# Batch norm on one core: loads and stores on two DMA rings, parameters in 16 equal rows, a shared last tile, and channels dealt 16 x 8 to the partitions

## The chip, the cores and the metric

One core of one Trainium2 chip. The metric is the device time of the kernel in microseconds (us), as the median of several runs. "The span" is the time from the first to the last record of one profiled execution; it is some 2 us shorter than the timed run. SBUF is the core's on-chip memory, rows of it are called partitions (128 of them); HBM is the large memory that x and the output lie in. A transfer (DMA) is cut into packets, here mostly one 64 KB row each, which 16 DMA engines carry; a ring is a queue of transfers for these engines (q1, SyncE's, and q10, ScalarE's, in the profiles). "In flight" means begun and not yet ended.

## The reference

```python
# x: (32, 256, 128, 128) float32; the parameters have one value per channel, shape (256,)
return gamma * (x - running_mean) / np.sqrt(running_var + 1e-5) + beta
```

Per channel this is one multiplication and one addition: `x * scale + shift`. x and the output have 536.9 MB each, so the kernel is a stream through the core.

## The kernel before

One image and 128 channels make a tile: 128 partitions x 16384 values, 64 KB per partition, 8.39 MB. There are 64 tiles and three buffers. All loads and stores are issued by SyncE, so they stand in one DMA ring (q1, 99.9% of the engines' span): three loads, three stores, three loads.

```python
NBUF = 3
GROUPS = [3] * 20 + [2, 2]
xr = x.rearrange("n (cb p) h w -> (n cb) p (h w)", p=P)          # partition p holds channel cb*128 + p
outr = out.rearrange("n (cb p) h w -> (n cb) p (h w)", p=P)

def load(i):
    t = data.tile([P, HW], f32, tag="t")
    nc.sync.dma_start(out=t[:], in_=xr[i])
    tiles[i] = t
# parameters: one row each, from ScalarE's ring, then a transpose and copies to 128 partitions
for r, ap in enumerate((running_var, gamma, beta, running_mean)):
    nc.scalar.dma_start(out=rows[r : r + 1, :], in_=ap.rearrange("(o c) -> o c", o=1))
# ... scale_t and shift_t from them: 12 small instructions (cut) ...
def compute(i):                       # in place, on VectorE
    nc.vector.tensor_scalar(out=t[:], in0=t[:], scalar1=scale_t[:, cb : cb + 1],
                            scalar2=shift_t[:, cb : cb + 1], op0=mult, op1=add)
first = 0
for g, size in enumerate(GROUPS):
    idxs = range(first, first + size)
    for i in idxs: compute(i)
    for i in idxs: store(i)           # nc.sync.dma_start(out=outr[i], in_=t[:])
    first += size
    for i in range(first, min(first + more, NT)): load(i)   # more: the size of the next group
```

Of the kernel before, what the change touches and what calls it, by code (L numbers as in the profile page):

```python
# [1 line left out]

# [4 lines left out]


NBUF = 3
GROUPS = [3] * 20 + [2, 2]  # L10

AHEAD = 0


@with_exitstack
def kernel(
    ctx: ExitStack,
    tc: tile.TileContext,
    x: bass.AP,
    gamma: bass.AP,  # L20
    beta: bass.AP,
    running_mean: bass.AP,
    running_var: bass.AP,
    out: bass.AP,
):
    nc = tc.nc
    eps = 1e-5
    f32 = mybir.dt.float32

    N, C, H, W = x.shape  # L30
    P = nc.NUM_PARTITIONS
    assert C % P == 0
    NCB = C // P
    HW = H * W
    NT = N * NCB
    B = 32
    NQ = P // B
    assert sum(GROUPS) == NT and max(GROUPS) <= NBUF

    params = ctx.enter_context(tc.tile_pool(name="params", bufs=1))  # L40
    data = ctx.enter_context(tc.tile_pool(name="data", bufs=NBUF))

    xr = x.rearrange("n (cb p) h w -> (n cb) p (h w)", p=P)
    outr = out.rearrange("n (cb p) h w -> (n cb) p (h w)", p=P)

    ctx.enter_context(tc.manual_schedule())
    tiles = {}

    def load(i):
        t = data.tile([P, HW], f32, tag="t")  # L50
        nc.sync.dma_start(out=t[:], in_=xr[i])  # L51
        tiles[i] = t


    rows = params.tile([B, C], f32, tag="rows")
    nc.vector.memset(rows, 0.0)  # L56
    for r, ap in enumerate((running_var, gamma, beta, running_mean)):
        nc.scalar.dma_start(out=rows[r : r + 1, :], in_=ap.rearrange("(o c) -> o c", o=1))

    for i in range(AHEAD + GROUPS[0]):  # L60
        load(i)

    eps_t = params.tile([P, 1], f32, tag="eps")
    nc.vector.memset(eps_t, eps)  # L64
    turned = params.tile([B, C], f32, tag="turned")
    nc.vector.transpose(out=turned[:], in_=rows[:])  # L66

    par = params.tile([P, NCB, 4], f32, tag="par")
    blocks = turned.rearrange("p (cb q r) -> p cb q r", cb=NCB, q=NQ)
    for q in range(NQ):  # L70
        nc.vector.tensor_copy(out=par[q * B : (q + 1) * B], in_=blocks[:, :, q, 0:4])  # L71
    var_t, gamma_t, beta_t, mean_t = (par[:, :, r] for r in range(4))

    scale_t = params.tile([P, NCB], f32, tag="scale")
    shift_t = params.tile([P, NCB], f32, tag="shift")
    tmp_t = params.tile([P, NCB], f32, tag="tmp")

    nc.scalar.activation(  # L78
        out=tmp_t[:],
        in_=var_t,  # L80
        func=mybir.ActivationFunctionType.Sqrt,
        bias=eps_t[:],
        scale=1.0,
    )
    nc.vector.reciprocal(out=tmp_t[:], in_=tmp_t[:])  # L85
    nc.vector.tensor_mul(out=scale_t[:], in0=gamma_t, in1=tmp_t[:])  # L86
    nc.vector.tensor_mul(out=tmp_t[:], in0=mean_t, in1=scale_t[:])  # L87
    nc.vector.tensor_sub(out=shift_t[:], in0=beta_t, in1=tmp_t[:])  # L88

    def compute(i):  # L90
        t = tiles[i]
        cb = i % NCB
        nc.vector.tensor_scalar(  # L93
            out=t[:],
            in0=t[:],
            scalar1=scale_t[:, cb : cb + 1],
            scalar2=shift_t[:, cb : cb + 1],
            op0=mybir.AluOpType.mult,
            op1=mybir.AluOpType.add,
        )  # L100

    def store(i):
        t = tiles.pop(i)
        nc.sync.dma_start(out=outr[i], in_=t[:])  # L104


    first = 0
    for g, size in enumerate(GROUPS):
        idxs = range(first, first + size)
        for i in idxs:  # L110
            compute(i)
        for i in idxs:
            store(i)
        first += size
        more = GROUPS[g + 1] if g + 1 < len(GROUPS) else 0
        for i in range(first + AHEAD, min(first + AHEAD + more, NT)):
            load(i)


# [1 line left out]
_INS = ['x', 'gamma', 'beta', 'running_mean', 'running_var']  # L121
_OUTS = [((32, 256, 128, 128), 'float32')]


# [23 lines left out]
```

## Time and profile before

| | before |
|---|---|
| time, median (all) | 2485.87 us (2485.76 to 2486.37; 2485.97 in the three runs that the prediction had) |
| VectorE busy | 566 us of 2483.6 |
| DMA | 99.9% of 16 engines' span, 432 GB/s |
| one 64 KB DMA packet, median | 2418 ns, loads and stores alike |
| tile load, issue to landing, median | 58.0 us (three stand in the ring) |

The large idle time of VectorE follows from the busy DMA. The lines and their reading are in the prediction.

### The profile page before, as it was taken

To read this page: it belongs to the slowest core of one execution; us is meant where nothing else is said; L and a number is where in the kernel's file an instruction comes from. 1 tells how busy PE (TensorE), PEld (TensorE's weight loads), DVE (VectorE), ACT (ScalarE), POOL (GpSimd) and SP (SyncE) were. 2 spreads that over 40 slices of the span, in tenths; PEclk is the share of its full clock that TensorE was granted. 3 is DMA by queue.
4 is the path that set the end of the run, shared out by engine and by line. 5 is a ranking of instruction groups with operands and counts; after the bars stand their busy time and mean duration, and the time that the engine had idled before them with its cause. 6 is when DMAs were issued, how large, how long until landed. Compare 5 with 4: busy or idle time off the path is not lost.

```text
span 2483.6 us, 383 instructions
## 1 busy us (share of the span) xinstructions
DVE 566.0 (23%) x75; ACT 1.6 (0%) x2; POOL 0.2 (0%) x4
## 2 busy tenths in 40 slices
DVE  3140404121221213140403121221213040403112
ACT  0000000000000000000000000000000000000000
POOL 0000000000000000000000000000000000000000
DMA  9999999999999999999999999999999999999999
GB/s 421 423 439 439 425 436 439 431 431 439 431 431 439 435 426 436 436 431 435 435 435 427 439 434 427 439 434 427 439 437 432 432 437 433 431 437 433 431 437 396
DMA packets 18442, 1073.77 MB, mean 432 GB/s; under 512 B 2052, under 2 KB 2056, under 8 KB 2056
## 3 DMA queue, kind: packets, MB, share of 16 engines
q1 hardware_dynamic: 18432, 1073.75, 99.9%
q14 instruction: 2, 0.02, 0.0%
q10 hardware_dynamic: 8, 0.00, 0.0%
HBM read 536.88 MB, written 536.87 MB: 432 GB/s over the span
## 4 chain that ended last, share of the span: by engine, by line
another core or an unknown queue 72%; DVE 22%; DMA 4%; issue 0%; DVEq 0%; SPq 0%
DVE t L93 22%; DMA t<-in_x_dram 4%; DVEq L93 0%; SPq L51 0%; SPq L104 0%
## 5 line engine op out<-in xcount | busy, mean ns | idle before, releaser
L93 DVE TENSOR_SCALAR t<-t,scale_t,shift_t 128x16384 f32<-128x16384 f32 x64 | 564.0, 8812 | 1863.9 <-DMA t<-in_x_dram 1863.8
L66 DVE STREAM_TRANSPOSE turned<-rows 32x256 f32<-32x256 f32 x1 | 0.4, 432 | 21.5 <-DMA rows<-in_running_mean_dram 21.5
L78 ACT ACT_TABLE_LOAD x1 | 1.3, 1283 | 2.6 <-issue 2.6
L71 DVE COPY par<-turned 32x8 f32<-32x8 f32 x4 | 0.6, 161 | 0.1
L56 DVE MEMSET rows<- 32x256 f32 x1 | 0.3, 272 | 0.8 <-PEq L132 0.8
L78 ACT ACTIVATE tmp_t<-par,eps_t 128x2 f32<-128x2 f32 x1 | 0.3, 297 | 20.0 <-DVE par L71 20.0
L85 DVE RECIPROCAL tmp_t<-tmp_t 128x2 f32<-128x2 f32 x1 | 0.2, 165 | 0.4 <-ACT tmp_t L78 0.4
L87 DVE TENSOR_TENSOR tmp_t<-par,scale_t 128x2 f32<-128x2 f32 x1 | 0.2, 161 | 0.0
L88 DVE TENSOR_TENSOR shift_t<-par,tmp_t 128x2 f32<-128x2 f32 x1 | 0.2, 161 | 0.0
L86 DVE TENSOR_TENSOR scale_t<-par,tmp_t 128x2 f32<-128x2 f32 x1 | 0.2, 160 | 0.0
L132 POOL MEMSET const-uint8-127<- 128x1 uint8 x1 | 0.1, 103 | 0.0
L132 POOL MEMSET const-bfloat16-1.0<- 128x1 bf16 x1 | 0.1, 101 | 0.0
L132 POOL MEMSET const-float32-0.0<- 128x1 f32 x1 | 0.1, 98 | 0.2 <-issue 0.2
L132 POOL MEMSET const-float32-1.0<- 128x1 f32 x1 | 0.1, 98 | 0.0
L64 DVE MEMSET eps_t<- 128x1 f32 x1 | 0.1, 59 | 0.0
## 6 DMA issues: line engine op xcount, KB each, us to landing
t<-in_x_dram SPq DMA_DIRECT2D x64, 58.0
out_dram<-t SPq DMA_DIRECT2D x64, 49.1
rows<-in_running_var_dram ACTq DMA_DIRECT2D x1, 1.0 KB
rows<-in_gamma_dram ACTq DMA_DIRECT2D x1, 1.0 KB
rows<-in_beta_dram ACTq DMA_DIRECT2D x1, 1.0 KB
rows<-in_running_mean_dram ACTq DMA_DIRECT2D x1, 1.0 KB
```

The lines of the kernel that those rows point to most:

```text
L56: nc.vector.memset(rows, 0.0)
L64: nc.vector.memset(eps_t, eps)
L66: nc.vector.transpose(out=turned[:], in_=rows[:])
L71: nc.vector.tensor_copy(out=par[q * B : (q + 1) * B], in_=blocks[:, :, q, 0:4])
L78: nc.scalar.activation(out=tmp_t[:], in_=var_t, func=mybir.ActivationFunctionType.Sqrt, bias=eps_t[:], scale=1.0,)
L85: nc.vector.reciprocal(out=tmp_t[:], in_=tmp_t[:])
L86: nc.vector.tensor_mul(out=scale_t[:], in0=gamma_t, in1=tmp_t[:])
L87: nc.vector.tensor_mul(out=tmp_t[:], in0=mean_t, in1=scale_t[:])
L88: nc.vector.tensor_sub(out=shift_t[:], in0=beta_t, in1=tmp_t[:])
L93: nc.vector.tensor_scalar(out=t[:], in0=t[:], scalar1=scale_t[:, cb : cb + 1], scalar2=shift_t[:, cb : cb + 1], op0=mybir.AluOpType.mult, ...
L132: nc = _bacc.Bacc("TRN2", target_bir_lowering=False, num_devices=1)
```

## The change

Its intent: (1) loads on SyncE's ring and stores on ScalarE's, so that neither stands behind the other; (2) each parameter row sent to 16 partitions, so that each engine has the same number of packets, behind the first half of tile 0; (3) the last tile shared by VectorE and ScalarE; (4) channels dealt so that partition 8e+k holds channel 16k+e: the 16 engines are meant to work on 16 adjacent rows of HBM at a time. Core of the diff:

```diff
-    xr = x.rearrange("n (cb p) h w -> (n cb) p (h w)", p=P)
-    outr = out.rearrange("n (cb p) h w -> (n cb) p (h w)", p=P)
+    NE = 16;  NK = P // NE
+    xr = x.rearrange("n (cb k e) h w -> (n cb) e k (h w)", k=NK, e=NE)
+    outr = out.rearrange("n (cb k e) h w -> (n cb) e k (h w)", k=NK, e=NE)
...
-        nc.scalar.dma_start(out=rows[r : r + 1, :], in_=ap.rearrange("(o c) -> o c", o=1))
+        nc.sync.dma_start(out=bufs[0][:, left], in_=xr[0][:, :, left]).then_inc(early, 16)
+            inst = nc.sync.dma_start(out=rows[0:NE, r * C : (r + 1) * C], in_=ap.partition_broadcast(NE))
+        nc.sync.dma_start(out=bufs[0][:, right], in_=xr[0][:, :, right]).then_inc(loaded[0], 16)
+        for i in range(1, NT):
+            s, turn = i % NBUF, i // NBUF
+            inst = nc.sync.dma_start(out=bufs[s][:], in_=xr[i]).then_inc(loaded[s], 16)
+            if turn:
+                inst._wait_ge(stored[s], 16 * turn)
...
+                out=lined.rearrange("p (rc e k) -> p rc e k", e=NE, k=NK),     # the parameters dealt likewise
+                in_=rows.rearrange("p (rc k e) -> p rc e k", k=NK, e=NE),
...
-        nc.sync.dma_start(out=outr[i], in_=t[:])
+            nc.scalar.dma_start(out=outr[i], in_=bufs[s][:])._wait_ge(done, after).then_inc(stored[s], 16)
...
+        compute(last, slice(0, VCOLS))          # VCOLS = 9216 of 16384 columns on VectorE
+        nc.scalar.activation(out=t[:, VCOLS:], in_=t[:, VCOLS:], func=Identity,
+                             bias=shift_t[:, cb : cb + 1], scale=scale_t[:, cb : cb + 1])
```

More of the change, by code (lines that the diff above doesn't have):

```diff
@@ L9 @@
 NBUF = 3
-GROUPS = [3] * 20 + [2, 2]
-AHEAD = 0
+VCOLS = 9216
 @with_exitstack
@@ L37 @@
     NQ = P // B
-    assert sum(GROUPS) == NT and max(GROUPS) <= NBUF
-    params = ctx.enter_context(tc.tile_pool(name="params", bufs=1))
-    data = ctx.enter_context(tc.tile_pool(name="data", bufs=NBUF))
-    xr = x.rearrange("n (cb p) h w -> (n cb) p (h w)", p=P)
-    outr = out.rearrange("n (cb p) h w -> (n cb) p (h w)", p=P)
-    ctx.enter_context(tc.manual_schedule())
-    tiles = {}
-    def load(i):
-        t = data.tile([P, HW], f32, tag="t")
-        nc.sync.dma_start(out=t[:], in_=xr[i])
-        tiles[i] = t
@@ L55 @@
-    rows = params.tile([B, C], f32, tag="rows")
-    nc.vector.memset(rows, 0.0)
-    for r, ap in enumerate((running_var, gamma, beta, running_mean)):
-        nc.scalar.dma_start(out=rows[r : r + 1, :], in_=ap.rearrange("(o c) -> o c", o=1))
-    for i in range(AHEAD + GROUPS[0]):
-        load(i)
-    eps_t = params.tile([P, 1], f32, tag="eps")
-    nc.vector.memset(eps_t, eps)
-    turned = params.tile([B, C], f32, tag="turned")
-    nc.vector.transpose(out=turned[:], in_=rows[:])
-    par = params.tile([P, NCB, 4], f32, tag="par")
@@ L69 @@
-    blocks = turned.rearrange("p (cb q r) -> p cb q r", cb=NCB, q=NQ)
-    for q in range(NQ):
-        nc.vector.tensor_copy(out=par[q * B : (q + 1) * B], in_=blocks[:, :, q, 0:4])
-    var_t, gamma_t, beta_t, mean_t = (par[:, :, r] for r in range(4))
-    scale_t = params.tile([P, NCB], f32, tag="scale")
-    shift_t = params.tile([P, NCB], f32, tag="shift")
-    tmp_t = params.tile([P, NCB], f32, tag="tmp")
-    nc.scalar.activation(
-        out=tmp_t[:],
-        in_=var_t,
-        func=mybir.ActivationFunctionType.Sqrt,
-        bias=eps_t[:],
-        scale=1.0,
-    )
@@ L85 @@
-    nc.vector.reciprocal(out=tmp_t[:], in_=tmp_t[:])
-    nc.vector.tensor_mul(out=scale_t[:], in0=gamma_t, in1=tmp_t[:])
-    nc.vector.tensor_mul(out=tmp_t[:], in0=mean_t, in1=scale_t[:])
-    nc.vector.tensor_sub(out=shift_t[:], in0=beta_t, in1=tmp_t[:])
-    def compute(i):
-        t = tiles[i]
-        cb = i % NCB
-        nc.vector.tensor_scalar(
-            out=t[:],
-            in0=t[:],
-            scalar1=scale_t[:, cb : cb + 1],
-            scalar2=shift_t[:, cb : cb + 1],
-            op0=mybir.AluOpType.mult,
-            op1=mybir.AluOpType.add,
-        )
@@ L102, in store @@
-    def store(i):
-        t = tiles.pop(i)
-        nc.sync.dma_start(out=outr[i], in_=t[:])
-    first = 0
-    for g, size in enumerate(GROUPS):
-        idxs = range(first, first + size)
-        for i in idxs:
-            compute(i)
-        for i in idxs:
-            store(i)
-        first += size
-        more = GROUPS[g + 1] if g + 1 < len(GROUPS) else 0
-        for i in range(first + AHEAD, min(first + AHEAD + more, NT)):
-            load(i)
+    NE = 16
+    NPAR = 4
+    NK = P // NE
@@ new lines @@
+    xr = x.rearrange("n (cb k e) h w -> (n cb) e k (h w)", k=NK, e=NE)
+    outr = out.rearrange("n (cb k e) h w -> (n cb) e k (h w)", k=NK, e=NE)
+    params = ctx.enter_context(tc.tile_pool(name="params", bufs=1))
+    data = ctx.enter_context(tc.tile_pool(name="data", bufs=1))
+    bufs = [data.tile([P, HW], f32, name=f"t{s}", tag=f"t{s}") for s in range(NBUF)]
+    rows = params.tile([B, NPAR * C], f32, name="rows", tag="rows")
+    lined = params.tile([B, NPAR * C], f32, name="lined", tag="lined")
@@ new lines @@
+    turned = params.tile([B, NPAR * C], f32, name="turned", tag="turned")
+    par = params.tile([P, NPAR, NCB], f32, name="par", tag="par")
+    eps_t = params.tile([P, 1], f32, name="eps_t", tag="eps")
+    std_t = params.tile([P, NCB], f32, name="std_t", tag="std")
+    rstd_t = params.tile([P, NCB], f32, name="rstd_t", tag="rstd")
+    scale_t = params.tile([P, NCB], f32, name="scale_t", tag="scale")
+    ms_t = params.tile([P, NCB], f32, name="ms_t", tag="ms")
+    shift_t = params.tile([P, NCB], f32, name="shift_t", tag="shift")
@@ new lines, with step, compute, store @@
+    loaded = [tc.alloc_semaphore(f"loaded{s}") for s in range(NBUF)]
+    stored = [tc.alloc_semaphore(f"stored{s}") for s in range(NBUF)]
+    early = tc.alloc_semaphore("early")
+    done = tc.alloc_semaphore("done")
+    fetched = tc.alloc_semaphore("fetched")
+    vec = tc.alloc_semaphore("vec")
+    act = tc.alloc_semaphore("act")
+    with tc.tile_critical():
+        count = [0]
+        def step(inst, sem=None, value=None):
+            if sem is not None:
+                inst._wait_ge(sem, value)
+            elif count[0]:
+                inst._wait_ge(vec, count[0])
+            inst.then_inc(vec, 1)
+            count[0] += 1
+            return count[0]
+        left, right = slice(0, HW // 2), slice(HW // 2, HW)
+        last = NT - 1
+        nc.sync.dma_start(out=bufs[0][:, left], in_=xr[0][:, :, left]).then_inc(early, 16)
+        zeroed = step(nc.vector.memset(rows[:], 0.0))
+        for r, ap in enumerate((running_var, gamma, beta, running_mean)):
+            inst = nc.sync.dma_start(out=rows[0:NE, r * C : (r + 1) * C], in_=ap.partition_broadcast(NE))
+            if r == 0:
+                inst._wait_ge(vec, zeroed)
+            inst.then_inc(fetched, 16)
+        nc.sync.dma_start(out=bufs[0][:, right], in_=xr[0][:, :, right]).then_inc(loaded[0], 16)
[4 more added lines that the diff above has]
+                inst._wait_ge(stored[s], 16 * turn)
+        step(nc.vector.memset(eps_t[:], eps))
+        step(
+            nc.vector.tensor_copy(
+                out=lined.rearrange("p (rc e k) -> p rc e k", e=NE, k=NK),
+                in_=rows.rearrange("p (rc k e) -> p rc e k", k=NK, e=NE),
+            ),
+            fetched,
+            16 * NPAR,
+        )
+        step(nc.vector.transpose(out=turned[:], in_=lined[:]))
+        blocks = turned.rearrange("p (rc q b) -> p rc q b", q=NQ, b=B)
+        flat = par.rearrange("p r cb -> p (r cb)")
+        for q in range(NQ):
+            placed = step(nc.vector.tensor_copy(out=flat[q * B : (q + 1) * B], in_=blocks[:, :, q, 0]))
+        var_t, gamma_t, beta_t, mean_t = (par[:, r] for r in range(NPAR))
+        nc.scalar.activation(
+            out=std_t[:],
+            in_=var_t,
+            func=mybir.ActivationFunctionType.Sqrt,
+            bias=eps_t[:],
+            scale=1.0,
+        )._wait_ge(vec, placed).then_inc(act, 1)
+        step(nc.vector.reciprocal(out=rstd_t[:], in_=std_t[:]), act, 1)
+        step(nc.vector.tensor_mul(out=scale_t[:], in0=gamma_t, in1=rstd_t[:]))
+        step(nc.vector.tensor_mul(out=ms_t[:], in0=mean_t, in1=scale_t[:]))
+        ready = step(nc.vector.tensor_sub(out=shift_t[:], in0=beta_t, in1=ms_t[:]))
+        nc.vector.wait_ge(vec, ready)
+        def compute(i, cols=slice(0, HW)):
+            t, cb = bufs[i % NBUF], i % NCB
+            return nc.vector.tensor_scalar(
+                out=t[:, cols],
+                in0=t[:, cols],
+                scalar1=scale_t[:, cb : cb + 1],
+                scalar2=shift_t[:, cb : cb + 1],
+                op0=mybir.AluOpType.mult,
+                op1=mybir.AluOpType.add,
+            ).then_inc(done, 1)
+        def store(i, after):
+            s = i % NBUF
+            nc.scalar.dma_start(out=outr[i], in_=bufs[s][:])._wait_ge(done, after).then_inc(stored[s], 16)
+        compute(0, left)._wait_ge(early, 16)
+        compute(0, right)._wait_ge(loaded[0], 16)
+        store(0, 2)
+        for i in range(1, last):
+            compute(i)._wait_ge(loaded[i % NBUF], 16 * (i // NBUF + 1))
+            store(i, i + 2)
+        turns = last // NBUF + 1
+        compute(last, slice(0, VCOLS))._wait_ge(loaded[last % NBUF], 16 * turns)
+        t, cb = bufs[last % NBUF], last % NCB
+        nc.scalar.activation(
+            out=t[:, VCOLS:],
+            in_=t[:, VCOLS:],
+            func=mybir.ActivationFunctionType.Identity,
+            bias=shift_t[:, cb : cb + 1],
+            scale=scale_t[:, cb : cb + 1],
+        )._wait_ge(loaded[last % NBUF], 16 * turns).then_inc(done, 1)
+        store(last, last + 3)
+        for s in range(NBUF):
+            nc.sync.wait_ge(stored[s], 16 * ((NT - s + NBUF - 1) // NBUF))
```

## The prediction

> **What bounds the kernel now.** I read the page's first three parts, then the timeline of the first and the last stretch, then the DMA packet records themselves. VectorE is busy for under a quarter of the span, ScalarE and GpSimd for nothing; one DMA ring is busy for all of it:
>
> ```profile
> span 2483.6 us, 383 instructions
> DVE 566.0 (23%) x75; ACT 1.6 (0%) x2; POOL 0.2 (0%) x4
> ...
> q1 hardware_dynamic: 18432, 1073.75, 99.9%
> ...
> q10 hardware_dynamic: 8, 0.00, 0.0%
> HBM read 536.88 MB, written 536.87 MB: 432 GB/s over the span
> ...
> L93 DVE TENSOR_SCALAR t<-t,scale_t,shift_t 128x16384 f32<-128x16384 f32 x64 | 564.0, 8812 | 1863.9 <-DMA t<-in_x_dram 1863.8
> ```
>
> q1 is SyncE's ring: 64 loads and 64 stores of 8.39 MB, 16384 data packets of 64 KB (one channel's row each) plus 2048 small ones that count completions (128 transfers x 16 engines). The 1863.8 us that VectorE waits for loads is not lost time: the DMA works all through it. The traffic cannot shrink either, as x is read once and out is written once (536.9 MB each). So the only question is how fast 16384 packets go through 16 engines, 1024 each, and how much is lost at the ends.
>
> The packet records (start, duration, bytes of each packet) answer the first half. The median duration of a 64 KB packet is 2418 ns, for loads and stores alike, and the 1st to the 95th percentile lie between 2418 and 2421 ns. Taken 16 at a time in order of start (one packet per engine), the starts lie 2414 to 2416 ns apart nearly everywhere. 65536 bytes in 2414.5 ns is 27.1 GB/s per engine, 434 GB/s for 16. A flat figure like that, the same in both directions, says that the engine's own data path is the limit, not HBM and not VectorE. The page's windows agree: 434 GB/s over a whole load-and-store round in the middle, less only at the ends.
>
> ```profile
> 0.00:62.00 62.00, 19.63 (x13) 1.58 (x2) 0.20 (x4) 1.00 1.00 420
> ...
> 1000.00:1116.00 116.00, 26.13 (x4) 0.00 (x0) 0.00 (x0) 1.00 1.00 434
> 2421.00:2484.00 63.00, 17.63 (x2) 0.00 (x0) 0.00 (x0) 1.00 0.90 392
> ```
>
> (The columns are length, busy us of VectorE, ScalarE and GpSimd, clock, DMA share, GB/s.) Now the sum of the span, from those records: 1.7 us to the first packet; 0.6 us by which the first packets are longer than the rest (mean 3.0 instead of 2.4 us); 1024 x 2.4145 = 2472.4 us; some 6 ns for each of 128 completions, 0.8 us; 1.5 us from the last packet to the end of the span. That is **2477.0**. The span is 2483.6, so only **6.6 us** are lost to anything a schedule can change. I find them in two places. (a) Where a group of three loads gives way to three stores, the packets at the switch are longer: 1.2 us per engine at the first switch (69 us), and on average 0.107 us per engine at the 19 that follow, 3.3 us in all; from stores to loads the mean is under 0.005 us. (b) These extras hit some engines more than others: the last data packets of the 16 engines end between 2477.9 and 2482.1 us, and the slowest one sets the end; against the mean that is 2 to 3 us.
>
> The two ends show that nothing else is exposed:
>
> ```profile
> 22.65 0.43 DVE L66 STREAM_TRANSPOSE turned<-rows 32x256 f32<-32x256 f32 x1 [21.53 <-DMA rows<-in_running_mean_dram]
> 24.95 8.81 DVE L93 TENSOR_SCALAR t<-t,scale_t,shift_t 128x16384 f32<-128x16384 f32 x1
> 33.80 37.81 SPq L104 DMA_DIRECT2D out_dram<-t  x3
> ...
> 2424.58 8.81 DVE L93 TENSOR_SCALAR t<-t,scale_t,shift_t 128x16384 f32<-128x16384 f32 x1 [49.09 <-DMA t<-in_x_dram]
> 2433.42 19.69 SPq L104 DMA_DIRECT2D out_dram<-t  x2
> 2443.92 8.81 DVE L93 TENSOR_SCALAR t<-t,scale_t,shift_t 128x16384 f32<-128x16384 f32 x1 [10.53 <-DMA t<-in_x_dram]
> ```
>
> The parameters land late (22.65 us) and the first store is queued at 33.8 us, but the ring is busy with three loads until about 60 us, so 26 us of that are slack. At the end the last tile lands at 2443.9 and its 8.81 us of VectorE lie beside the store of tile 62, which the ring carries until about 2463. The last tile's store is queued at 2452.8, ten microseconds before the engines are free for it.
>
> [...] 8 small packets on q10, alternating with 2.4 us packets of q1, make 19.3 us, and the parameters landed at 22.65, about 20 us after their issue. [...] an issue takes 0.34 us and none leaves the engines idle. [...]
>
> **The change part by part.**
> 1. *Parameters.* They move from one engine of q10 to all 16 of q1, behind the left half of tile 0. Per engine: four packets of 1 KB (one took 46 ns) and four completions (9 ns), about 0.22 us more DMA on 15 engines. They land after 8 packets of 32 KB, at about 2 + 8 x 1.21 + 2 = 13 to 14 us instead of 22.65. Then 32 x 1024 elements instead of 32 x 256: the rearranging copy and the transpose about 1.2 us each (estimate: 0.43 us for 256 columns, of which about 0.27 scale with them, times four), the small operations as before, 2.3 us: scale and shift are ready near 19 us rather than 25. All in slack; worth 0.
> 2. *Tile 0 in halves.* Eight more packet starts and one completion per engine, under 0.1 us. The first store can start near 28 us instead of 69; as the engines are busy in either case, 0.
> 3. *Two rings.* Loads on SyncE, stores on ScalarE, a buffer reloaded as soon as its store has landed. Does DMA ever run dry? A buffer's round is load 38.6 us (half rate beside a store), landing and VectorE and issue about 12, store 38.6, landing and issue about 2: 91 us, against 6 x 19.3 = 116 us of DMA work per round of three buffers. 25 us to spare, so one ring always has work. The gaps of (a) at whole-group switches vanish as such, but every packet now changes direction, about 500 load-to-store switches per engine instead of 21.
> 4. *Dealing the channels.* Same packets, same bytes, other order. In lock step the 16 engines are on one contiguous megabyte of HBM at a time. It may remove the uneven stretching of (b); at most part of the 6.6 us.
> 5. *Shared last tile.* VectorE does 9216 of 16384 columns, 8.81 x 0.5625 = 5.0 us, ScalarE the rest in about 6 us [...]. It stays hidden behind store 62, which still has up to 19 us to go; 0.
>
> Sum: floor 2477.0 + 0.3 of added packets. I keep some 4 to 5 us of stretching and skew under constantly mixed traffic, for a span near 2481.5. The timed median lies 2.4 us above the span before (2485.97 against 2483.6), so about **2484 us**, 0.1% less.
>
> **The rivals.**
> - *Each change of direction costs.* If each of about 500 load-to-store switches cost the average 0.107 us, that is 53 us: 2537 us, just over 2% slower. For it: the cost is seen at the switches and nowhere else. Against: it is no fixed cost. At the third switch none of 16 engines shows it, at the fourth 4 of 16, at the last 1, and the opposite switch is free. A tenth to a half of it gives 2490 to 2510.
> - *SBUF ports shared by two engines.* Two engines in the same direction on one port at once would stretch both packets, up to double in the worst case, far over 2600 us. [...] Against: load and store packets alternate, and a read and a write need not collide. I give it one in twenty-five.
> - *It becomes really faster.* 2% is 50 us, and 434 GB/s at 2418 ns per packet leave 6.6. Only a packet shorter than 2418 ns could do it, and the 16384 of before have none.
> - *A smooth gain.* All stretching and skew go: 2480 us.
>
> **Range and chances.** The low end is the floor of about 2477 + 0.3 + 2.4 = 2480, less a little if the second ring hides a few ns per packet: 2477. The high end covers a third of the first rival and some more: 2518. Faster by 2%: 0.01. Slower by 2%: the full first rival or the second: 0.10. Within 2%: 0.89.
>
> **What would show it right or wrong.** Right: q1 and q10 each carry half the bytes with a summed share near 99.9%; 434 GB/s in the middle; the 64 KB packets stay near 2418 ns; VectorE waits for loads throughout; the end follows the last store by 1.5 us. Where packets of both rings lie over each other, their durations double and only the rate counts. The first rival shows as a lower rate in the middle, evenly over all slices; the second as a much lower one. A slice in which the DMA share falls, with a ring waiting for VectorE or for a store, would refute the arithmetic of part 3; a last slice clearly below 392 GB/s, that of part 5.

2477.0 + 0.3 + some 4 to 5 us of stretching and skew make a span near 2481.5, and 2.4 more the 2484 us. Two things stand as the suppositions they were: that the flat 2418 ns show the engine's own data path as the limit, and that there are "ports" that engines can share. The traces show only which partitions slow each other, and by how much (experiment 4).

## The result, and the profile after

The changed kernel takes **3406.15 us** (median of 4 runs, 3349.89 to 3488.46) against 2485.87 us. Ratios here are the mean time of one kernel's fast runs over that of the other's fast runs of the same rounds, so not quite the ratio of the medians; this one is 1.353 (95% interval 1.344 to 1.362). The forecast was 2484 us. Executions over 1.5% slower than the fastest of the same kernel are left out of the means. Two of the four runs (3349.89 and 3376.39) count as fast; the profiled one, 3435.92 us, does not, but the experiments below show the same picture in fast runs.

The page of the changed kernel:

```profile
DVE 565.1 (16%) x77; ACT 7.9 (0%) x3; POOL 0.2 (0%) x4
...
DMA  9999999999999999999999999999999999999998
GB/s 236 300 326 317 334 324 332 334 305 316 336 323 318 311 311 294 292 296 289 297 292 299 312 307 334 336 309 318 338 327 331 326 306 318 318 326 327 329 343 220
...
q1 hardware_dynamic: 9488, 536.94, 60.0%
q10 hardware_dynamic: 9216, 536.88, 39.6%
```

The engines are as busy as before, the two rings share the bytes equally, and yet mostly 290 to 340 GB/s get through instead of 434, the much lower rate that the prediction had named as the sign of its second rival. The engines were not short of work: the packets themselves have become longer. Loads (q1) hold the engines for 60% of the span, stores (q10) for 40%, so a load packet takes longer than a store packet. The packet records say the same: 64 KB loads take 4.01 us on average and stores 2.66 us, where both took 2.42.

The first 43 us tell most, because only loads are in flight there. The timeline of the changed kernel, then its windows (length, busy us of VectorE, ScalarE, GpSimd, clock, DMA share, GB/s):

```profile
25.67 1.01 DVE L104 COPY lined<-rows 32x1024 f32<-32x1024 f32 x1 [23.42 <-DMA rows<-in_running_mean_dram]
...
49.56 58.15 ACTq L145 DMA_DIRECT2D out_dram<-t  x2
```

```profile
3.00:43.00 40.00, 8.09 (x11) 0.30 (x1) 0.00 (x0) 1.00 0.99 203
60.00:1000.00 940.00, 158.63 (x18) 0.00 (x0) 0.00 (x0) 1.00 1.00 322
```

203 GB/s with loads alone is a little under half of 434. The first 128 packets of 32 KB took 2.51 us on average where half of a 64 KB packet would be 1.21. Before the first store is even issued, at 49.6 us, the rate is already halved. So neither stores in the second ring nor any change of direction are needed for it. From then on, with loads and stores mixed, the rate is higher, not lower.

### The profile page after: what moved, and what is told of

The parts are those of the page before. It is cut to its first block, busy times and chain, and to the rows that moved or that the text cites. A ratio compares the mean times of both kernels' runs of the same rounds, so it can differ in the third digit from the quotient of the medians.

```text
span 3434.1 us, 267 instructions
## 1 busy us (share of the span) xinstructions
DVE 565.1 (16%) x77; ACT 7.9 (0%) x3; POOL 0.2 (0%) x4
## 4 chain that ended last, share of the span: by engine, by line
another core or an unknown queue 81%; DVE 16%; DMA 1%; ACT 0%; issue 0%; SPq 0%; ACTq 0%; DVEq 0%
DVE t L134 16%; DMA t<-in_x_dram 1%; ACT t L157 0%; SPq L91 0%; DVE rows L89 0%; ACTq L145 0%; DVE eps_t L102 0%; DVEq L193 0%; SPq L70 0%
## 5 line engine op out<-in xcount | busy, mean ns | idle before, releaser
L134 DVE TENSOR_SCALAR t<-t,scale_t,shift_t 128x16384 f32<-128x16384 f32 (+2 forms) x65 | 560.6, 8624 | 2792.5 <-DMA t<-in_x_dram 2792.3
```

The source lines that it names most:

```text
L134: return nc.vector.tensor_scalar(out=t[:, cols], in0=t[:, cols], scalar1=scale_t[:, cb : cb + 1], scalar2=shift_t[:, cb : cb + 1], op0=myb ...
```

## The experiments

Theories: **D-SBUF**, the dealing makes two engines meet at partitions that share one rate (the texts call what such partitions share a port; which partitions slow each other is measured in 4); **D-HBM**, 16 adjacent rows meet on one part of HBM; **R**, the second ring and its changes of direction cost. Every kernel below gave the reference's result.

### 1. The change without the dealing

```diff
-    xr = x.rearrange("n (cb k e) h w -> (n cb) e k (h w)", k=NK, e=NE)      # outr likewise
+    xr = x.rearrange("n (cb p) h w -> (n cb) p (h w)", p=P)                 # outr likewise
-                out=lined.rearrange("p (rc e k) -> p rc e k", e=NE, k=NK),
-                in_=rows.rearrange("p (rc k e) -> p rc e k", k=NK, e=NE),
+                out=lined[:], in_=rows[:],
```

> The changed kernel without the dealing: two rings, equal parameter rows and the shared last tile stay, but each load and store is the plain 128-row pattern again. Theory D (the dealing alone costs): back to 2477 to 2490 us, 64 KB packets near 2.42 us in both rings. Theory R (two rings cost, each change of direction): stays over 2540 us, in the extreme near the 3400 of the changed kernel.

Measured: median 2493.68 us, in two groups: 2483.97, 2483.99, 2484.74 and 2502.63, 2507.45, 2509.13; the second lies above the 2490 that I expected. Ratio to before 1.0040 (1.0007 to 1.0073). Its profile, taken in the lower group:

```profile
q1 hardware_dynamic: 9488, 536.94, 50.0%
q10 hardware_dynamic: 9216, 536.88, 49.9%
...
HBM read 536.94 MB, written 536.87 MB: 432 GB/s over the span
```

The 64 KB packets take 2421.7 ns (loads) and 2418.3 ns (stores) on average, although each engine changes between the rings hundreds of times (pieced together from the starts and ends of the packets, as the records do not name the engine). The dealing alone costs the 900 us, and R is refuted as their cause: in this run a load-to-store switch between two rings costs nothing that shows. What separates the two groups is taken up in 5.

### 2. The dealing alone, on one ring

```diff
 # the kernel before
-    xr = x.rearrange("n (cb p) h w -> (n cb) p (h w)", p=P)                 # outr likewise
+    xr = x.rearrange("n (cb k e) h w -> (n cb) e k (h w)", k=8, e=16)       # outr likewise
+    nc.vector.tensor_copy(out=lined..., in_=rows...)                        # the parameters dealt likewise
```

> The kernel before, with only the channels dealt 16 x 8 (one ring, groups of three loads and three stores). Theory D-port, both directions alike (two engines share an SBUF port for reads and for writes): all packets about 4.8 us, some 4900 us. Theory D-write (only writing into SBUF is shared at half rate): loads about 5.1 us a packet as at the start of the changed kernel, stores about 2.5 to 2.7, some 512 x 5.1 + 512 x 2.6 = 3950 us. Theory R: close to 2490 us.

Measured: 4518.15 us (4501.11 and 4535.19), ratio 1.816. Windows of this kernel, at the start (loads only) and over a thousand microseconds:

```profile
3.00:63.00 60.00, 10.90 (x11) 1.23 (x2) 0.00 (x0) 1.00 1.00 208
...
1000.00:2000.00 1000.00, 123.38 (x14) 0.00 (x0) 0.00 (x0) 1.00 1.00 240
```

The first 24 packets per engine, all loads, take 5.03 us on average; the next 24, all stores, 4.39. So stores suffer too, and my "write only" variant falls. 4518 lies between my two figures (4900 and 3950): 69% of all packets take over 4.5 us, 14% take under 2.5 us, near the plain 2.42. And the second ring, far from being the cause, *saves* some 1100 us of the damage (3406 against 4518).

### 3. Dealt, but not to adjacent rows; and dealt 32 x 4

```diff
 # the changed kernel; rings_far: engines on rows 1 MB apart, SBUF side as in the change
-    xr = x.rearrange("n (cb k e) h w -> (n cb) e k (h w)", k=NK, e=NE)
+    xv = x.rearrange("n (e cb k) h w -> n cb e k (h w)", cb=NCB, e=NE)
 # rings_deal32: 32 blocks of 4 partitions instead of 16 blocks of 8
-    NK = P // NE
+    NK = 4;  ND = P // NK        # and e=ND in the four patterns
```

> The changed kernel with another dealing: partition 8e+k holds channel 16e+8cb+k, so the pattern is still 16 x 8 with the same SBUF side, but the 16 engines work on HBM rows 1 MB apart instead of adjacent ones. Theory D-SBUF (which partitions an engine serves decides): as slow as the changed kernel, 3300 to 3500 us, first loads 2.1 times the plain time. Theory D-HBM (16 adjacent rows meet on the same part of HBM): back to 2480 to 2550 us.

> The changed kernel with the channels dealt 32 x 4 instead of 16 x 8: partition 4e+k holds channel 32k+e. If any 2-level pattern hands each engine eight consecutive partitions (split by blocks in order)[...]: 3250 to 3500 us. If the engine is picked per block of four partitions [...]: 2480 to 2510 us, 64 KB packets at 2.42 us.

Measured: rings_far 3345.37 us (3251.71, 3344.02, 3346.73, 3464.79; only the first counts as fast, so no ratio is given), rings_deal32 2484.26 us (2483.75 to 2503.37), ratio 1.0018 (0.9990 to 1.0046). Lines of rings_far, its page and the window of its loads alone, then of the page of rings_deal32:

```profile
q1 hardware_dynamic: 9488, 536.94, 58.1%
q10 hardware_dynamic: 9216, 536.88, 41.7%
...
HBM read 536.94 MB, written 536.87 MB: 330 GB/s over the span
...
3.00:43.00 40.00, 7.90 (x12) 0.29 (x1) 0.00 (x0) 1.00 1.03 213
```

```profile
GB/s 407 439 436 426 439 436 431 434 436 436 429 436 439 426 436 439 431 432 438 436 428 436 439 427 435 439 431 433 437 437 428 436 439 427 435 439 431 433 436 394
```

Moving the rows apart in HBM changes nothing in kind (loads alone at 213 GB/s against 203, the rings split 58 to 42 against 60 to 40): D-HBM falls. Dealing in blocks of four partitions instead of eight gives the full rate back (433 GB/s over the span), and neighbouring blocks still hold adjacent rows of HBM. Of these two dealings it is thus the number of consecutive partitions under one step of the outer dimension that decides. I had named both outcomes for rings_deal32.

### 4. Chosen partitions by themselves

Two kernels put small transfers in front of the kernel of experiment 1: stages of three DMAs, each partition one 64 KB packet, every stage waiting for the one before. In the stages of 4 or 16 partitions each packet has an engine of its own: the DMA shares of 0.23 to 0.25 and 0.95 to 0.97 below are 4 and 16 busy engines of 16.

```diff
+PROBES = [  # partitions, rows, step between the rows in DRAM, first row, store instead of load
+    (slice(0, 128), 128, 1, 0),       (slice(0, 4), 4, 1, 0),           (slice(0, 13, 4), 4, 1, 0),
+    (slice(0, 97, 32), 4, 1, 0),      (slice(0, 25, 8), 4, 1, 0),       (slice(0, 4), 4, 100, 0),
+    (slice(0, 13, 4), 4, 100, 0),     (slice(0, 121, 8), 16, 1, 0),     (slice(0, 121, 8), 16, 8, 0),
+    (slice(0, 4), 4, 1, 0, True),     (slice(0, 13, 4), 4, 1, 0, True), (slice(0, 121, 8), 16, 1, 0, True)]
 # second kernel, SBUF to SBUF: first partition and step it reads, first partition and step it writes
+PROBES = [((0, 4), (16, 4)), ((0, 4), (32, 4)), ((0, 1), (16, 4)), ((0, 4), (16, 1)), ((0, 1), (32, 1)), ((0, 8), (32, 8))]
```

> rings_plain with twelve stages of three small DMAs each in front of it, every stage waiting for the one before, each partition a 64 KB packet on its own engine (4 or 16 engines). Durations of the packets. Theory D-SBUF [...]: 128 plain rows 2.42 us; partitions 0-3 (one port) 9.7; 0,4,8,12 (four ports) 2.42; 0,32,64,96 (two ports) 4.8; 0,8,16,24 (four ports) 2.42; 0-3 from rows 100 apart 9.7; 0,4,8,12 from rows 100 apart 2.42; 0,8,..,120 adjacent rows 4.8; the same from rows 8 apart 4.8; stores from 0-3 9.7, from 0,4,8,12 2.42, from 0,8,..,120 4.8 (under D-write all three stores near 2.42 to 2.7). Theory D-HBM: only the rows matter, stages with adjacent rows slow, stages with rows 8 or 100 apart 2.42, whatever the partitions. After the stages the kernel runs as rings_plain.

> rings_plain with six stages of SBUF-to-SBUF copies of 4 rows of 64 KB in front, to see whether a read and a write at one SBUF port share its rate. [...] Read 0,4,8,12 write 16,20,24,28 [...]: 2.42 us a packet. Read 0,4,8,12 write 32,36,40,44 [...]: 2.42 if reading and writing have their own rate, 4.8 if they share one. Read 0-3 (one port) write 16,20,24,28: 9.7 to 10.2. Read 0,4,8,12 write 16-19: 9.7 to 10.2. Read 0-3 write 32-35 [...]: about 10 if separate, about 20 if shared. Read 0,8,16,24 write 32,40,48,56: 2.42 or 4.8, as the second. [...] What follows is rings_plain once more: its time less the stages should be near 2484 or near 2505 us, the two levels seen before.

The expected durations are multiples of the 2.42 us of one packet: four, two or one engines at partitions that I took to share one rate.

Windows of the first kernel, one per stage (the last number is GB/s over the stage, its start and end included):

```profile
1.90:61.30 59.40, 0.28 (x2) 0.28 (x1) 0.00 (x0) 1.00 0.99 424
62.40:91.50 29.10, 0.00 (x0) 0.00 (x0) 0.00 (x0) 1.00 0.24 27
93.90:102.40 8.50, 0.00 (x0) 0.00 (x0) 0.00 (x0) 1.00 0.23 93
103.80:119.00 15.20, 0.00 (x0) 0.00 (x0) 0.00 (x0) 1.00 0.24 52
...
130.90:158.60 27.70, 0.00 (x0) 0.00 (x0) 0.00 (x0) 1.00 0.25 28
...
171.70:187.60 15.90, 0.00 (x0) 0.00 (x0) 0.00 (x0) 1.00 0.96 198
189.50:205.30 15.80, 0.00 (x0) 0.00 (x0) 0.00 (x0) 1.00 0.95 199
206.70:237.60 30.90, 0.00 (x0) 0.00 (x0) 0.00 (x0) 1.00 0.25 25
239.20:246.70 7.50, 0.00 (x0) 0.00 (x0) 0.00 (x0) 1.00 0.24 105
248.00:263.70 15.70, 0.00 (x0) 0.00 (x0) 0.00 (x0) 1.00 0.97 200
```

In order: the plain 128 rows at 424 GB/s; four engines on partitions 0-3, 27 GB/s for all four together (9.7 to 10.1 us a packet in the settled second and third DMA of the stage); on 0, 4, 8, 12, 93 GB/s (2.42 us); on 0, 32, 64, 96, 52 GB/s (5.0 us); on 0-3 from rows 100 apart in HBM, 28 again; sixteen engines on 0, 8, .., 120, 198 GB/s (5.12 us), the same from rows 8 apart, 199; stores from 0-3, from 0, 4, 8, 12 and from 0, 8, .., 120: 25, 105 and 200 GB/s. (The stages 0, 8, 16, 24 and 0, 4, 8, 12 from rows 100 apart, not shown, settle at 2.42 us.) So four engines on 0-3 share about the rate of one undisturbed packet (65536 bytes in 2.42 us are 27.1 GB/s); engines on 0, 4, 8, 12, or on 0, 8, 16, 24, share nothing that shows; and each engine on 0, 32, 64, 96, or on 0, 8, .., 120, has about half the rate, as if it shared with one other. Which two of these share, and what it is that they share, the stages do not show. HBM rows play no part (28 against 27 GB/s, 199 against 198), and stores are slowed on the same partitions as loads (25, 105 and 200 GB/s against 27, 93 and 198). The sixteen partitions in steps of eight are also the ones that the 16 x 8 dealing would have in flight first if each engine had eight consecutive partitions: 5.12 us here, 5.03 for the loads at the start of experiment 2.

The second kernel copies from SBUF to SBUF. Its six stages:

```profile
62.70:70.10 7.40, 0.00 (x0) 0.00 (x0) 0.00 (x0) 1.00 0.25 106
71.60:79.00 7.40, 0.00 (x0) 0.00 (x0) 0.00 (x0) 1.00 0.25 106
80.50:111.20 30.70, 0.00 (x0) 0.00 (x0) 0.00 (x0) 1.00 0.25 26
112.80:140.20 27.40, 0.00 (x0) 0.00 (x0) 0.00 (x0) 1.00 0.25 29
143.30:174.00 30.70, 0.00 (x0) 0.00 (x0) 0.00 (x0) 1.00 0.25 26
175.60:183.00 7.40, 0.00 (x0) 0.00 (x0) 0.00 (x0) 1.00 0.25 106
```

Stage 2 (reads 0, 4, 8, 12, writes 32, 36, 40, 44) runs like stage 1 (the same reads, writes 16, 20, 24, 28). Stage 5 reads 0-3 and writes 32-35: 26 GB/s, the same as stage 3, which reads 0-3 too but writes 16, 20, 24, 28; one rate for all eight would have made it 13. So four writes to 32-35 cost these reads no more than four spread writes. That reading and writing at one and the same group of partitions do not share a rate would follow only if 32-35 belonged to one group with 0-3; I had assumed that, and the stage 0, 32, 64, 96 allows it but does not show it. How the second ring softens the damage is therefore not shown. My estimate is that an engine that loads and one that stores slow each other less than two that load; the windows of the changed kernel agree with it (322 GB/s with loads and stores mixed, 203 with loads alone). The expectation's other half, the timed remainder of this kernel, decides nothing: a single run, 2693.86 us with the stages.

### 5. The two levels of the plain two-ring kernel

```diff
 # plain_oldparams: rings_plain with the parameters as before, one row on one engine
+            inst = nc.scalar.dma_start(out=rows[0:1, r * C : (r + 1) * C], in_=ap.rearrange("(o c) -> o c", o=1))
 # one_ring_rest: rings_plain with one ring, groups of three loads and three stores
-            nc.scalar.dma_start(out=outr[i], in_=bufs[s][:])...       # after each compute
+            nc.sync.dma_start(out=outr[i], in_=bufs[s][:])...         # three loads, then three stores
 # deal32_tail: rings_deal32 with the last tile loaded, computed and stored in two column halves
```

> rings_plain with the parameters fetched as in the kernel before: one row each, from ScalarE's ring, on one engine alone. If equal parameter rows keep the engines in step and so keep the time at 2484 us, this one should lie at the higher level, about 2505 us, more often than rings_plain (3 of 6 runs). If the parameters are in slack, as predicted: the same two levels, median between 2482 and 2510 us.

> rings_plain with one ring again: loads and stores all from SyncE in groups of three as in the kernel before; equal parameter rows, halved first tile and shared last tile stay. If the second ring is what makes half of rings_plain's runs 20 us longer: all runs within 2 us of one another, 2482 to 2488 us. If the longer runs come from the parameters or the last tile, they show here too.

> rings_deal32 unchanged, on another chip, as the measure for the run beside it and to count how often the higher level comes: runs near 2484 us and near 2503 us, some 30 to 50% of the higher ones.

> rings_deal32 with the last tile loaded, computed and stored in two column halves. In the one higher-level trace at hand (plain_oldparams, 2503 us) some engines still had load packets of the last tile while the others had run out of stores, so the last tile's compute and store waited for the latest engine and about 12 us of DMA lay idle. If that exposed wait is the cause of the higher level, half of the last tile can be stored meanwhile and the higher runs fall to about 2487 to 2495 us; the lower ones stay at 2484 to 2485. If the higher level comes from longer packets all through, nothing changes: 2484 and 2503 to 2516 us.

| kernel | runs, us | ratio to before (95%) |
|---|---|---|
| plain_oldparams | 2483.29, 2483.3, 2503.23, 2506.59, 2511.33, 2515.9 | 1.0059 (1.0020 to 1.0097) |
| one_ring_rest | 2485.58, 2487.29, 2487.77, 2487.85, 2488.17 | 1.0005 (0.9993 to 1.0017) |
| deal32_again | 2483.6, 2484.01, 2484.87, 2485.23, 2490.28 | 0.9997 (0.9985 to 1.0009) |
| deal32_tail | 2487.22, 2488.95, 2497.51, 2501.68, 2502.66, 2504.93 | 1.0043 (1.0021 to 1.0066) |

With one ring, in groups of three again, and all the rest of the change but the dealing, the runs stay within 2.6 us of one another and equal the kernel before: the spread belongs to the second ring and the order that comes with it, and parameters and shared last tile are worth nothing. Two of six runs with the old parameters lie at the lower level and three of six with the new: equal rows were not shown to help. In deal32_again I expected 30 to 50% of the runs near 2503 us; none of the five was.

The profiled run of plain_oldparams fell in the higher level. Windows and the start of the last tile from its end, then from the end of rings_plain in the lower level:

```profile
2425.00:2450.00 25.00, 8.81 (x1) 0.00 (x0) 0.00 (x0) 1.00 1.01 433
2450.00:2475.00 25.00, 1.94 (x1) 1.94 (x1) 0.00 (x0) 1.00 0.70 301
2475.00:2500.00 25.00, 3.14 (x1) 4.42 (x1) 0.00 (x0) 1.00 0.80 343
...
2473.06 6.36 ACT L157 ACTIVATE t<-t,shift_t,scale_t 128x7168 f32<-128x7168 f32 x1 [2455.96 <-DMA t<-in_x_dram]
```

```profile
2425.00:2450.00 25.00, 0.00 (x0) 0.00 (x0) 0.00 (x0) 1.00 1.02 443
2450.00:2475.00 25.00, 5.08 (x1) 6.36 (x1) 0.00 (x0) 1.00 0.97 419
...
2452.97 6.36 ACT L157 ACTIVATE t<-t,shift_t,scale_t 128x7168 f32<-128x7168 f32 x1 [2435.64 <-DMA t<-in_x_dram]
```

In the higher level the DMA falls to 0.70 while the last tile is waited for. The packet records show the wait: its 16 last load packets end between 2451.0 and 2470.3 us, 19 us apart, in the lower level between 2447.4 and 2450.1. The likely reading is that the engines no longer go in step, so that some reach the end with stores done and loads left. The last tile waits for the latest of them (ScalarE and VectorE start at 2473.1), while the others have nothing to do. Summed over the run the packets are also longer, by about 10 us per engine (2489.3 us of packet time against 2479.1), most of it in the second half. Of the 18.4 us between the two spans (2501.4 and 2483.0) some 8 are then left for the wait at the end.

The remedy that follows from this, halving the last tile, failed: its runs reach from 2487 to 2505 us, which fits neither of my two forecasts (all runs within 2484 to 2495, or nothing changed). In its profiled run (2497.5 us) the last load packets still end 10 us apart, and the DMA share falls to 0.80 from 2450 to 2475 us. With one trace at the higher level, the exposed wait is seen as a part of it; what makes the packets longer and takes the engines out of step in some runs, and why the halved tail has more of it, stays open.

## Why the prediction was wrong

- **The step that failed is part 4, "Dealing the channels. Same packets, same bytes, other order."** The packets have the same bytes but not the same duration: 4.01 us per load and 2.66 per store instead of 2.42. The mis-sized term is 1024 x 2.4145 = 2472.4 us: in the profiled run the packets of x and the output took 3419 us per engine, of a span of 3434. Behind the step stood the reading "the engine's own data path is the limit". The flat 2418 ns did show one steady limit; it did not show that the limit was the engine's. Four engines on partitions 0-3 together got 27 GB/s too (experiment 4), the 27.1 of one engine by itself, so from flat packets alone a limit of the engine and a limit of the partitions cannot be told apart.
- **The rival with one chance in twenty-five fits best.** That engines which meet "would stretch both packets, up to double in the worst case" is what experiments 2, 3 and 4 support: about half the rate with loads alone (208 GB/s against 424), the same with other HBM rows (213), none of it with 32 x 4 (433 over the span), and 5.0 to 5.1 us a packet instead of 2.42 on partitions 0, 32, 64, 96 and on 0, 8, .., 120, all loads. That in the 16 x 8 dealing each engine serves eight consecutive partitions is an inference, as the packet records do not name the engine. I had discounted the rival with "load and store packets alternate, and a read and a write need not collide". In the plain two-ring kernel they did not (2421.7 and 2418.3 ns), and in the dealt one the second ring takes the factor from 1.82 to 1.35, but a loss of 35% remains. That the engines which meet are not always in opposite phases would account for it; this was not measured. Why loads bear more of it than stores is not settled.
- **The rival that got most of the weight, a cost per change of direction, is not what happened:** hundreds of changes per engine, packets of 2418 to 2422 ns on average (experiment 1, lower level), so the doubling that the prediction expected where packets of both rings lie over each other did not show either. At the higher level the packets are some 10 us longer per engine, a fifth of that rival's 53 us, and most such runs lie in the 2490 to 2510 us that "a tenth to a half of it" would give; whether the changes of direction cause this is not shown.
- **Right, once the dealing is taken out:** 2484.0 us at the lower level against 2484 predicted, though the median over both levels is 2493.7 (inside the range). Some of the match is luck: the 2.4 us between span and timed run compared two executions, while within the profiled run they lie 1.75 us apart (2485.35 and 2483.6), and the span is 2483.0 against 2481.5. Right too are the parameters behind the half tile (the wait for them ends at 14.3 us against 13 to 14), scale and shift at 18.1 (near 19), first store at 28.0 (near 28), ScalarE's share of the last tile 6.36 us (about 6). Adjacent rows won nothing: at the lower level 2484.0 us without them (experiment 1) and 2484.2 with them (rings_deal32).
- **Part 5, "stays hidden behind store 62", held at the lower level only,** where the last load packets end 2.7 us apart. At the higher level (19 us apart) the last tile is exposed, as the test I had named says (the last slice of the page has 330 GB/s, well below 392).

No version beats the kernel before clearly. The two-ring kernel dealt 32 x 4 comes to 2484 or 2485 us in most runs (0.1% less) and to 2490 or 2503 in some; one ring is steadier.

## What to carry to other kernels

The pattern of a 128-partition transfer can change its rate while packets and bytes stay the same. Before reshaping one into an outer and an inner dimension, measure it with one direction alone: blocks of four partitions kept the full rate here (433 GB/s over the span), blocks of eight halved it (203 to 208 GB/s with loads alone, against 424). When a busy share stays at 99% while the time grows, compare packet durations and look at a stretch with one direction alone: here the first 40 us held the answer.
